# A two-layer float32 encoder trunk on one core: queueing edges in the second MLP product of layer 0 and in the attention output product, one weight cast moved ahead, and one activation table set for a norm's root and the softmax

## The chip, the core and the metric

The kernel runs on one core of one Trainium2 chip. The core has a matrix engine (TensorE; in the profile PE, its weight loads PEld), a vector engine (VectorE, DVE), an engine for activation functions and copies (ScalarE, ACT), a general engine (GpSimd, POOL) and an engine that only issues transfers (SyncE, SP). Each engine works through its own list of instructions in order; an instruction that depends on another engine waits on a semaphore, and everything behind it on the same engine waits too. The metric is the device time of one execution in microseconds (us).

## The reference

Two sequences of 512 tokens with 1024 features, `x_prompt` and `x_sample`, go through the same trunk. All is float32. Layer 0 mixes tokens with a 2-D Fourier transform and a product with `w_out`; layer 1 is attention with 8 query heads that share 2 key/value heads of 128 features. Each mixer is followed by an MLP with a squared ReLU.

```python
for i in range(2):
    if i == 0:
        x = x + fourier_mix(rms_norm(x, fourier_norm), fourier_w_out)
    else:
        x = x + gqa_attention(rms_norm(x, attn_norm), w_qkv, q_norm, k_norm, w_o)
    x = x + sq_relu_mlp(rms_norm(x, mlp_norm[i]), mlp_w_up[i], mlp_w_down[i])   # 1024 -> 4096 -> 1024
y = rms_norm(x, final_norm)

def rms_norm(x, g):
    return x * rsqrt(mean(x * x, axis=-1) + 1e-6) * g

def gqa_attention(h, w_qkv, q_gain, k_gain, w_o):     # per head
    q, k = axial_rope(rms_norm(q, q_gain)) * 128 ** -0.5, axial_rope(rms_norm(k, k_gain))
    return concat(softmax(q @ k.T) @ v) @ w_o
```

## The kernel before

**Products.** Each float32 operand is split into two reduced-precision halves: the high half is a cast on ACT (`split`, line 86; the page writes CAST L86), the low half is the difference to the source, a subtraction on DVE (line 87). A product is three matmuls: high by high, high by low, low by high (`mm3`, lines 81 to 83, in attention; `product`, line 907, elsewhere). Where float32 weights arrive by DMA, the tile is `raw`, its halves `w`; for activations both are `u`. PSUM banks are `ps`, eight of them. `halves` splits a whole weight tile of 128x1024 and returns two operands of 512 columns.

**Blocks.** Activations are kept transposed: features on partitions, tokens along the free axis. The MLP products and the product with W_o use Strassen's scheme over a 2x2 division (the two sequences are one of the divided sides): seven products of sums of blocks instead of eight. The class `Blocks` prepares the operands for the next layer's products: `gain` (line 206, ACT, multiplies by the norm's weight), `root` and `spread` (sums of squares, their root, and the root spread over partitions), `norm` (line 219, DVE, multiplies by the root), `first` (line 230, ACT, the high half) and `first_lo` (line 235, DVE, the low half), and `plain_sums` for the sums of blocks. `square` (lines 160 and 164) squares a feature block on ACT and adds it on POOL to a running sum.

**The order of a run.** The Fourier layer comes first; at its end (loop around line 870) every step adds one product to the residual, squares and scales it, and in some steps the MLP's first weight tiles are split. Then comes layer 0's first MLP product (`first_product`, results to DRAM), then its second (`second_product`), attention, W_o, layer 1's MLP and the final norm. Residuals that are not in use wait in DRAM (`park`; `put_away` writes, SP issues it).

**The second MLP product** works through items (a feature block m of four, a group of hidden rows g). In an item, PE runs the products of `Row` and `Sums`; meanwhile the weights of the next item are summed and split: after the product t3 the rows' casts, after t2 `sum_23` and `split_12`, after b22 `sum_4` and `split_4`, after t4 `split_3`, which makes the last pair of halves that the next item needs. When a block m has had its last item, `finish` adds the shared sum `e` to the residual (lines 1253 and 1254) and calls `ready(m)`. In layer 0, `ready` makes the attention layer's input (`make_h`: ACT line 90, DVE line 91), squares it, and puts the residual away.

**Attention.** `qkv` makes projections, `norm_rope` normalises each head of q and k by its root mean square and rotates it. The root comes from `rsqrt_steps`: Sqrt on ACT (line 136), a reciprocal and one Newton step on DVE. For the very last q tile, `norm_rope` is called with POOL as one of its engines; its steps are spread over the first heads. A loop over 16 heads then takes, for head n, four score tiles (`scores`: three matmuls, maximum on DVE, Exp on ACT line 1474, reciprocal on DVE, scaling on POOL), alternating with the transposition of the head before (`transpose_p`: four transposes on PE line 1482, a split on ACT and DVE), then transposes the next q (`transpose_q`, line 1461), then multiplies by the values (`values`; line 1499 copies the result). From the seventh head on, `load_kept` also loads and splits the first four W_o tiles, one half per step (line 1568): 8 halves. ACT needs a table for each function: a page's ACT_TABLE_LOAD is the load of one. After the loop, line 1682 issues a Sqrt whose only use is that its table is there for layer 1.

**The product with W_o** has a first, a middle and a last part; the last one takes the operands t1 and b22, adds each product to the residual (`add`, line 1688), squares and scales it, and between these begins the MLP's preparation for sequence 0: `root(0)`, `spread(0)`, `first(0)` to `first(3)`, `first_lo(0)` and `first_lo(1)`.

**What sets the order.** Inside `tc.manual_schedule(engines=...)` the named engines run in the order of the program text. Everywhere else a scheduler takes instructions by the order of the program and the modelled availability of their inputs, so the order on an engine can differ from that of the text. The Fourier loop above is ordered so, and so are ACT, DVE and POOL in the second MLP product and in the heads (there PE too); in the last part of W_o only PE follows the text. A dependency between two instructions can be added by hand; it then constrains this scheduler.

Of the kernel before, what the change touches and what calls it, by code (L numbers as in the profile page):

```python
# [19 lines left out]
P = 128  # L20
# [24 lines left out]
def trunk_kernel(ctx, tc, x_in, xt_in, y_out, tables, rope, gfour, gcol, grow, gfin,  # L45
# [39 lines left out]
    def split(dst_hi, dst_lo, src, eng=nc.vector):  # L85
        nc.scalar.copy(dst_hi, src)  # L86
        eng.tensor_sub(dst_lo, src, f32(dst_hi))  # L87
# [18 lines left out]
    def halves(raw, n=512, home=own):  # L106
        hi, lo = home()
        split(hi[:, : 2 * n], lo[:, : 2 * n], raw)
        return [(hi[:, i * n : (i + 1) * n], lo[:, i * n : (i + 1) * n]) for i in range(2)]
# [34 lines left out]

    xs, acc, apart = {}, {}, {}
# [9 lines left out]
    def square(q, fo, n=512, alone=False, first=0):  # L155

        if fo == first:
            acc[q] = tm()
        s = acc[q] if fo == first else tm()
        nc.scalar.activation(s[:, :n], xt(q, fo)[:, :n], AF.Square)  # L160
        if alone:
            apart[q] = s
        elif fo != first:
            nc.gpsimd.tensor_add(acc[q][:, :n], acc[q][:, :n], s[:, :n])  # L164

# [29 lines left out]
    class Blocks:  # L195
# [37 lines left out]
        def first_lo(self, i):  # L233
            h = self.b["b11" if i < 2 else "b21"][i % 2]
            nc.vector.tensor_sub(h[1], self.f[0, i], f32(h[0]))  # L235
# [466 lines left out]
    with tc.manual_schedule(engines={ET.PE, ET.Activation, ET.DVE, ET.Pool, ET.SP}):  # L702
# [163 lines left out]
        for fo in range(KC):  # L866
            odd_add(1, fo, odd_outs(1, [fo])[0])
            if fo == 7:
                rows.append(halves(raws[3]))
            if fo:  # L870
# [7 lines left out]
            if fo == 5:  # L878
                rows.append(halves(raws[2]))
# [214 lines left out]
    def second_product(l, blocks, rows, late=lambda: None, ready=lambda m: None):  # L1094
        e, new = [], [True] * 4
        there = set()
# [72 lines left out]
        class Sums:  # L1169
# [27 lines left out]
            def split_3(self):  # L1197
                self.s3, self.a22 = halves(self.y, self.n * P, (own, narrow)[self.n == 2])
# [51 lines left out]
        def finish(m):  # L1250
            left[m] -= 1
            if left[m] == 0:
                nc.vector.tensor_add(xs[0, m][:, 1], xs[0, m][:, 1], e[m])
                nc.vector.tensor_add(xs[1, m], xs[1, m], e[m].unsqueeze(1).broadcast_to([P, 2, 512]))
                ready(m)
# [107 lines left out]
    def ready(m):  # L1363
        for q in range(NSEQ):
            for fo in range(2 * m, 2 * m + 2):
                hT[q].append(make_h(q, fo, KC))
                square(q, fo)
            put_away(q, m)

# [32 lines left out]
    def norm_rope(raw, nh, table, ts, outs, ss=None, step=None, eng=nc.vector, scale=None):  # L1402
# [9 lines left out]
        steps = rsqrt_steps(r[:, :n], ss[:, :n], n, 1.0 / HD)  # L1412
# [32 lines left out]
    heads_out, ahead = Blocks(None), []  # L1445
# [33 lines left out]
    def transpose_p(probs, sc):  # L1479
# [4 lines left out]
        split(k[:, 0], k[:, 1], pt)  # L1484
        return k
# [65 lines left out]
    def load_kept():  # L1551
# [14 lines left out]
        for j in range(2 if i < 4 else 0):  # L1566
            yield
            split(*ahead[i][j], raw[:, j * 512 : j * 512 + 512])
# [79 lines left out]
    with tc.manual_schedule(engines={ET.Activation}):  # L1648
        o = qkv(1, 1, 2, ws[1])
        probs = [scores(*heads[0], first, t) for t in range(NT)]  # L1650
# [11 lines left out]
    for n in range(1, len(heads) + 1):  # L1662
        pts, nxt = [], []
        for t in range(NT):
            if n < len(heads):
                nxt.append(scores(*heads[n], qT, t))
            pts.append(transpose_p(probs, t))
# [19 lines left out]
    def add(x, o):  # L1687
        nc.vector.tensor_add(x, o, x)
# [9 lines left out]
    with tc.manual_schedule(engines={ET.PE}):  # L1698
# [38 lines left out]
        o = {}  # L1737
        for j, (m, i) in enumerate(turn()):
# [4 lines left out]
            add(xt(1, fo), o[m])  # L1743
# [10 lines left out]
            if 2 < j < 5:  # L1754
                blocks.first_lo(j - 3)
# [293 lines left out]
```

## Time and profile before

| | |
|---|---|
| three plain runs | 1680.02, 1680.24, 1682.67 us (median 1680.24) |
| profiled execution | 1682.5 us; its span 1680.5 us |
| instructions | 22279 |
| PE busy | 1666.0 us, 99% (7845 matmuls) |
| DVE busy | 1258.9 us, 75% |
| ACT busy | 873.4 us, 52% |
| POOL busy | 394.5 us, 23% |
| HBM | 218.11 MB read, 82.38 MB written, 179 GB/s over the span |

The span is the time from the first to the last instruction of the profiled execution; the execution's own time is 2.0 us longer. The table gives shares over the whole run, and says nothing of a single stage. A timeline row begins with the time at which a group of like instructions begins (us from the span's start), then their busy time, the engine, the line of the kernel, the operation, output and input tiles with their shapes, and the count; a bracket at the end gives idle time just before and what ended it. "u<-ps" is a tile u written from a PSUM bank.

Some places of this execution: the third Fourier weight tile (edit 1 below) is cast at 96.55 us, the last residual add of block 2 in layer 0 (edit 2) begins at 694.04, the activation table loads in the heads (edit 3) begin at 865.25 and 869.27, and the last part of W_o (edit 6) stands near 1046.

### The profile page before, as it was taken

To read this page: it belongs to the slowest core of one execution; us is meant where nothing else is said; L and a number is where in the kernel's file an instruction comes from. 1 tells how busy PE (TensorE), PEld (TensorE's weight loads), DVE (VectorE), ACT (ScalarE), POOL (GpSimd) and SP (SyncE) were. 2 spreads that over 40 slices of the span, in tenths; PEclk is the share of its full clock that TensorE was granted. 3 is DMA by queue.
4 is the path that set the end of the run, shared out by engine and by line. 5 is a ranking of instruction groups with operands and counts; after the bars stand their busy time and mean duration, and the time that the engine had idled before them with its cause. 6 is when DMAs were issued, how large, how long until landed. Compare 5 with 4: busy or idle time off the path is not lost.

```text
span 1680.5 us, 22279 instructions
## 1 busy us (share of the span) xinstructions
PE 1666.0 (99%) x7845; PEld 1387.7 (83%) x7845; DVE 1258.9 (75%) x1848; ACT 873.4 (52%) x1537; POOL 394.5 (23%) x364
## 2 busy tenths in 40 slices
PE   9999999999999999999999999999999999999998
PEld 8988888888888888788878888888888888888887
DVE  8879776557786779869888877777855487878865
ACT  6766444456343425447698854554544553433334
POOL 3321443221000001325544303004422220000002
PEclk9999999999999999999999999999999999999999
DMA  9843655459775757425501146334544696757532
GB/s 310 262 151 111 209 194 182 145 176 371 242 231 170 254 171 225 168 65 196 168 1 39 63 164 224 124 114 160 209 156 155 226 367 203 232 158 237 176 102 100
DMA packets 122047, 302.99 MB, mean 180 GB/s; under 512 B 12200, under 2 KB 13352, under 8 KB 121936
## 3 DMA queue, kind: packets, MB, share of 16 engines
q1 hardware_dynamic: 98576, 254.05, 43.6%
q0 software_dynamic: 8960, 21.05, 5.9%
q10 hardware_dynamic: 14400, 26.48, 4.2%
q8 instruction: 61, 1.00, 0.2%
q14 instruction: 50, 0.41, 0.1%
HBM read 218.11 MB, written 82.38 MB: 179 GB/s over the span
## 4 chain that ended last, share of the span: by engine, by line
PE 87%; DVE 6%; ACT 3%; issue 2%; DMA 2%; POOL 0%; SPq 0%; DVEq 0%; ACTq 0%; POOLq 0%
PE ps L907 69%; PE ps L83 5%; PE ps L81 5%; PE ps L82 5%; PE ps L1482 1%; DVE w L87 1%; ACT t L1474 1%; ACT u L86 1%; DVE u L87 1%; DVE u L219 1%; DVE u L235 1%; DVE u L1113 0%; DMA u<-w_four 0%; DMA u<-x 0%; PE ps L172 0%
## 5 line engine op out<-in xcount | busy, mean ns | idle before, releaser
L907 PE MATMUL ps<-u,w 128*128 128x512 f32 x4944 | 1133.3, 390 | 2.9 <-DVE w L87 2.1
L907 PEld LDWEIGHTS ps<-u,w 128*128 128x128 f32 x4944 | 927.5, 188 | 199.1 <-DVE w L87 3.2
L86 ACT CAST w<-raw 128x1024 fp32r<-128x1024 f32 (+1 forms) x216 | 214.0, 996 | 310.9 <-PE ps L907 229.0
L87 DVE TENSOR_TENSOR w<-raw,w 128x1024 fp32r<-128x1024 f32 (+1 forms) x216 | 252.3, 1172 | 77.6 <-ACT w L86 77.3
L86 ACT CAST u<-u 128x1024 fp32r<-128x1024 f32 x144 | 145.2, 1049 | 83.8 <-PE ps L907 36.5
L87 DVE TENSOR_TENSOR u<-u,u 128x1024 fp32r<-128x1024 f32 x144 | 173.3, 1230 | 19.0 <-ACT u L86 17.9
L907 PE MATMUL ps<-u,u 128*128 128x512 f32 x600 | 143.1, 389 | 0.1
L1142 POOL DMA_DIRECT2D raw<-w_sum x32 | 27.7, 866 | 469.3 <-DMA raw<-w_sum 197.9
L1113 DVE TENSOR_TENSOR u<-ps,u 128x512 f32<-128x512 f32 x160 | 109.6, 686 | 37.2 <-PE ps L907 34.4
L1023 POOL TENSOR_TENSOR u<-u 128x512 f32<-128x512 f32 x28 | 37.7, 1345 | 424.7 <-ACT u L920 424.7
L907 PEld LDWEIGHTS ps<-u,u 128*128 128x128 f32 x600 | 112.5, 188 | 23.8 <-ACT u L938 0.5
L81 PE MATMUL ps<-u,u 128*128 128x512 f32 (+2 forms) x340 | 128.8, 381 | 0.4 <-ACT t L1474 0.3
L82 PE MATMUL ps<-u,u 128*128 128x512 f32 (+2 forms) x340 | 124.2, 366 | 0.4 <-DVE u L87 0.3
L83 PE MATMUL ps<-u,u 128*128 128x512 f32 (+2 forms) x340 | 124.4, 366 | 0.1
L164 POOL TENSOR_TENSOR t<-t,t 128x512 f32<-128x512 f32 (+1 forms) x54 | 77.8, 1446 | 190.6 <-ACT t L160 189.9
L919 ACT ACTIVATE t<-t 128x512 f32<-128x512 f32 x64 | 40.5, 632 | 109.8 <-DVE t L992 99.8
L87 DVE TENSOR_TENSOR u<-ps,u 128x512 fp32r<-128x512 f32 (+3 forms) x112 | 68.5, 635 | 7.9 <-ACT u L86 7.3
L83 PEld LDWEIGHTS ps<-u,u 128*128 128x128 f32 x340 | 64.2, 189 | 10.5 <-DVE u L448 0.5
L81 PEld LDWEIGHTS ps<-u,u 128*128 128x128 f32 x340 | 64.3, 189 | 10.1 <-ACT u L86 1.5
L82 PEld LDWEIGHTS ps<-u,u 128*128 128x128 f32 x340 | 64.4, 189 | 9.2 <-DVE u L87 1.4
L979 DVE TENSOR_TENSOR t<-ps,u 128x512 f32<-128x512 f32 x32 | 22.0, 688 | 60.5 <-PE ps L907 52.7
L1476 POOL TENSOR_SCALAR t<-t,s 128x512 f32<-128x512 f32 x64 | 47.3, 740 | 74.0 <-DVE s L1475 60.1
(260 smaller groups left out, 2029.7 us busy)
## 6 DMA issues: line engine op xcount, KB each, us to landing
raw<-w_up SPq DMA_DIRECT2D x80, 512.0 KB, 4.6
u<-spill_t SPq DMA_DIRECT2D x60, 512.0 KB, 6.8
raw<-w_sum SPq DMA_DIRECT2D x56, 512.0 KB, 5.7
u<-spill_b SPq DMA_DIRECT2D x45, 512.0 KB, 6.2
spill_t<-u SPq DMA_DIRECT2D x84, 256.0 KB, 2.0
spill_b<-t ACTq DMA_DIRECT2D x60, 256.0 KB, 4.3
raw<-w_row SPq DMA_DIRECT2D x28, 512.0 KB, 5.2
park<-u SPq DMA_DIRECT2D x24, 512.0 KB, 4.5
```

Source lines behind the costliest of these rows:

```text
L81: nc.tensor.matmul(out, lh, rh, start=first, stop=False)
L82: nc.tensor.matmul(out, lh, rl, start=False, stop=False)
L83: nc.tensor.matmul(out, ll, rh, start=False, stop=last)
L86: nc.scalar.copy(dst_hi, src)
L87: eng.tensor_sub(dst_lo, src, f32(dst_hi))
L164: nc.gpsimd.tensor_add(acc[q][:, :n], acc[q][:, :n], s[:, :n])
L907: nc.tensor.matmul(o, w[x][:, sl], h[k][y], start=first and k + i == 0, stop=k == n - 1 and i == 2, skip_group_check=not first)
L919: nc.scalar.activation(t, src, AF.Relu)
L1023: eng.tensor_sub(t[:, 0], b12, b11)
L1113: nc.vector.tensor_add(x, o, x)
L1142: nc.gpsimd.dma_start(s[:, 1], w[:, 3], accum_op=ALU.add)
L1476: nc.gpsimd.tensor_scalar(p, p, sm_[:, :1], 1.0, ALU.mult, ALU.mult)
```

## The change

It has six edits.

1. At the end of the Fourier layer the split of the third weight tile, `halves(raws[2])` at step 5, stands ahead of that step's square and gain instead of behind them.
2. `behind(x, y)` is a new helper: instruction x may only come after y, as an order (no semaphore) or, with `sync=True`, as a wait. In `second_product` of layer 0, when block m = 2 is finished, the last residual add (line 1254) is placed behind the low half that the next item's `split_3` makes last, and six squares (the last two of block 1, and block 2's four) are placed behind the same low half with a wait.
3. A new `log_steps` computes the root by Ln and Exp(-0.5 x) instead of Sqrt and a reciprocal, with the same Newton step; `norm_rope` uses it in the one call that names POOL.
4. Before the first softmax the table set that holds both Ln and Exp is loaded.
5. The splits of W_o's first four tiles in the heads are remembered in `fresh`; one is taken at the fourth `transpose_p` of a head and placed behind that transposition's own split, cast behind cast and subtraction behind subtraction.
6. In the last part of W_o the low halves of `first_lo(0)` and `first_lo(1)` are placed behind the residual adds of steps 4 and 5.

To allow this, `split`, `square`, `first_lo`, `ready` and `add` return the instructions that they issue, and `halves` takes a function to be called with its low half.

```diff
@@ -83,8 +83,14 @@
         nc.tensor.matmul(out, ll, rh, start=False, stop=last)
 
     def split(dst_hi, dst_lo, src, eng=nc.vector):
-        nc.scalar.copy(dst_hi, src)
-        eng.tensor_sub(dst_lo, src, f32(dst_hi))
+        hi = nc.scalar.copy(dst_hi, src)
+        return hi, eng.tensor_sub(dst_lo, src, f32(dst_hi))
+
+    def behind(x, y, sync=False):
+
+        kind = mybir.DependencyClass.Sync if sync else mybir.DependencyClass.NoSync
+        tc.add_manual_dep(x.ins, y.ins.name, mybir.DependencyInfo(kind, mybir.DependencyReason.SCHED_ONLY),
+                          reason="order")
 
     def split_scaled(dst_hi, dst_lo, src, scale):
         nc.scalar.activation(dst_hi, src, AF.Copy, scale=scale)
@@ -103,9 +109,9 @@
         w = slot([P, 2, 512], F32R)
         return w[:, 0], w[:, 1]
 
-    def halves(raw, n=512, home=own):
+    def halves(raw, n=512, home=own, done=lambda x: None):
         hi, lo = home()
-        split(hi[:, : 2 * n], lo[:, : 2 * n], raw)
+        done(split(hi[:, : 2 * n], lo[:, : 2 * n], raw)[1])
         return [(hi[:, i * n : (i + 1) * n], lo[:, i * n : (i + 1) * n]) for i in range(2)]
 
     def lent():
@@ -142,6 +148,18 @@
 
 
 
+    def log_steps(out, ss, n, inv):
+
+        v, s, r, t = [small(n)[:, :n] for _ in range(4)]
+        return [
+            lambda: nc.vector.tensor_scalar(v, ss, inv, EPS, ALU.mult, ALU.add),
+            lambda: nc.scalar.activation(s, ss, AF.Ln, scale=inv, bias=eps[:, :1]),
+            lambda: nc.scalar.activation(r, s, AF.Exp, scale=-0.5),
+            lambda: nc.vector.tensor_mul(t, r, r),
+            lambda: nc.vector.scalar_tensor_tensor(t, t, -0.5, v, ALU.mult, ALU.mult),
+            lambda: nc.vector.scalar_tensor_tensor(out, t, 1.5, r, ALU.add, ALU.mult),
+        ]
+
     xs, acc, apart = {}, {}, {}
 
     def load_xs(q, src):
@@ -157,11 +175,12 @@
         if fo == first:
             acc[q] = tm()
         s = acc[q] if fo == first else tm()
-        nc.scalar.activation(s[:, :n], xt(q, fo)[:, :n], AF.Square)
+        made = nc.scalar.activation(s[:, :n], xt(q, fo)[:, :n], AF.Square)
         if alone:
             apart[q] = s
         elif fo != first:
             nc.gpsimd.tensor_add(acc[q][:, :n], acc[q][:, :n], s[:, :n])
+        return made
 
     def sums(q, n=NT):
 
@@ -232,7 +251,7 @@
 
         def first_lo(self, i):
             h = self.b["b11" if i < 2 else "b21"][i % 2]
-            nc.vector.tensor_sub(h[1], self.f[0, i], f32(h[0]))
+            return nc.vector.tensor_sub(h[1], self.f[0, i], f32(h[0]))
 
         def plain_sums(self):
 
@@ -867,6 +886,8 @@
             odd_add(1, fo, odd_outs(1, [fo])[0])
             if fo == 7:
                 rows.append(halves(raws[3]))
+            if fo == 5:
+                rows.append(halves(raws[2]))
             if fo:
                 square(1, fo - 1)
             if fo > 1:
@@ -875,8 +896,6 @@
                 rows.append(halves(raws[fo]))
             if 1 < fo < 4:
                 blocks.first_lo(fo)
-            if fo == 5:
-                rows.append(halves(raws[2]))
         square(1, KC - 1)
         for fo in range(KC - 2, KC):
             gain1(fo)
@@ -1093,7 +1112,7 @@
 
     def second_product(l, blocks, rows, late=lambda: None, ready=lambda m: None):
         e, new = [], [True] * 4
-        there = set()
+        there, owed = set(), []
 
         def fetch(op, g, n):
 
@@ -1195,7 +1214,8 @@
                 split(*self.s4, self.x[:, 0])
 
             def split_3(self):
-                self.s3, self.a22 = halves(self.y, self.n * P, (own, narrow)[self.n == 2])
+                self.s3, self.a22 = halves(self.y, self.n * P, (own, narrow)[self.n == 2],
+                                           lambda x: setattr(self, "low", x))
 
             def go(self, i):
                 m, x0, x1 = self.m, xs[0, self.m], xs[1, self.m]
@@ -1251,8 +1271,14 @@
             left[m] -= 1
             if left[m] == 0:
                 nc.vector.tensor_add(xs[0, m][:, 1], xs[0, m][:, 1], e[m])
-                nc.vector.tensor_add(xs[1, m], xs[1, m], e[m].unsqueeze(1).broadcast_to([P, 2, 512]))
-                ready(m)
+                x = nc.vector.tensor_add(xs[1, m], xs[1, m], e[m].unsqueeze(1).broadcast_to([P, 2, 512]))
+                made = ready(m)
+                if m == 1 and made:
+                    owed.extend(made[2:])
+                if m == 2 and made:
+                    behind(x, items[-1][1].low)
+                    for y in owed + made:
+                        behind(y, items[-1][1].low, True)
 
         first_product(l, blocks, rows, ahead)
         e += [tm() for _ in range(4)]
@@ -1361,11 +1387,13 @@
         split(*wkv[-1], raw)
 
     def ready(m):
+        made = []
         for q in range(NSEQ):
             for fo in range(2 * m, 2 * m + 2):
                 hT[q].append(make_h(q, fo, KC))
-                square(q, fo)
+                made.append(square(q, fo))
             put_away(q, m)
+        return made
 
     second_product(0, blocks, rows, late, ready)
 
@@ -1409,7 +1437,7 @@
             head_squares(raw, 0, n, ss, 1.0 if scale is None else scale)
             yield
         r = small(n)
-        steps = rsqrt_steps(r[:, :n], ss[:, :n], n, 1.0 / HD)
+        steps = (log_steps if eng is nc.gpsimd else rsqrt_steps)(r[:, :n], ss[:, :n], n, 1.0 / HD)
         steps[0]()
         yield
         steps[1]()
@@ -1442,7 +1470,7 @@
             yield
 
     vt, kr, kT, qr = {}, {}, {}, {}
-    heads_out, ahead = Blocks(None), []
+    heads_out, ahead, fresh = Blocks(None), [], []
 
     def transpose_k(q):
         for h in range(NKV):
@@ -1481,8 +1509,7 @@
         for t in range(NT):
             nc.tensor.transpose(pt[:, t * P : (t + 1) * P], probs[t][:, sc * P : (sc + 1) * P], ident)
         k = slot([P, 2, 512], F32R)
-        split(k[:, 0], k[:, 1], pt)
-        return k
+        return k, split(k[:, 0], k[:, 1], pt)
 
     def values(q, h, pts):
         o = ps()
@@ -1565,7 +1592,7 @@
         ahead.append([(w[0][:, c : c + 512], w[1][:, c : c + 512]) for c in (0, 512)])
         for j in range(2 if i < 4 else 0):
             yield
-            split(*ahead[i][j], raw[:, j * 512 : j * 512 + 512])
+            fresh.append(split(*ahead[i][j], raw[:, j * 512 : j * 512 + 512]))
 
 
     transposes = {(0, 0, 0): 0, (0, 1, 0): 1}
@@ -1647,6 +1674,7 @@
     raw, ss = slot([P, 1024], F32), small(8)
     with tc.manual_schedule(engines={ET.Activation}):
         o = qkv(1, 1, 2, ws[1])
+        tc.keep_in_program_order(nc.scalar.preload_act_table_set("natural_log_exp_and_others"))
         probs = [scores(*heads[0], first, t) for t in range(NT)]
         nc.scalar.activation(raw[:, :512], o, AF.Copy, scale=rs[1][:, 2:3])
         qT = transpose_q(*heads[1])
@@ -1664,7 +1692,12 @@
         for t in range(NT):
             if n < len(heads):
                 nxt.append(scores(*heads[n], qT, t))
-            pts.append(transpose_p(probs, t))
+            k, both = transpose_p(probs, t)
+            pts.append(k)
+            if t == NT - 1:
+                for x in (fresh.pop() if fresh else ()), :
+                    for a, b in zip(x, both):
+                        behind(a, b)
             if n > 2 and t == 0:
                 for _ in range(3 if n == 3 else 1):
                     next(todo, None)
@@ -1685,7 +1718,7 @@
     load_xs(0, park[0])
 
     def add(x, o):
-        nc.vector.tensor_add(x, o, x)
+        return nc.vector.tensor_add(x, o, x)
 
     def turn(*steps):
 
@@ -1734,13 +1767,15 @@
                 next(todo, None)
                 if k == 2 and m < 2:
                     rows.append(halves(load_raw(w_up[1, 2 * m]), home=lent))
-        o = {}
+        o, lows = {}, []
         for j, (m, i) in enumerate(turn()):
             if i == 0:
                 o[m] = ps()
             product(o[m], ahead[10 + m][i], heads_out.operand(("t1", "b22")[i]), i == 0)
             fo = 2 * m + 1 - i
-            add(xt(1, fo), o[m])
+            added = add(xt(1, fo), o[m])
+            if 3 < j < 6:
+                behind(lows[j - 4], added)
             square(1, fo, first=1)
             blocks.gain(1, fo)
             if i:
@@ -1752,7 +1787,7 @@
             if 1 < j < 6:
                 blocks.first(j - 2)
             if 2 < j < 5:
-                blocks.first_lo(j - 3)
+                lows.append(blocks.first_lo(j - 3))
         for i in range(2, 4):
             blocks.first_lo(i)
     second_product(1, blocks, rows)
```

## The prediction

> **What bounds the kernel now.** I read the page first, then PE's busy time, matmuls and clock in chosen stretches, then the timeline of each engine where PE falls behind.
>
> ```profile
> span 1680.5 us, 22279 instructions
> PE 1666.0 (99%) x7845; PEld 1387.7 (83%) x7845; DVE 1258.9 (75%) x1848; ACT 873.4 (52%) x1537; POOL 394.5 (23%) x364
> ```
>
> PE bounds the kernel: it is busy for 1666.0 of 1680.5 us. No part of the change takes a matmul away, so only PE's waits can be gained, and 14.5 us of idle time, with what hides in overlapping records, is all there is. Matmul records overlap, so the counts show what busy time hides.
>
> ```profile
> 120.00:160.00 40.00, 40.00 (x176) 1.00 0.22 79
> 697.70:701.10 3.40, 3.40 (x9) 0.50 0.90 241
> 851.06:866.51 15.45, 15.45 (x90) 1.00 0.01 2
> 866.51:884.00 17.49, 16.72 (x91) 1.00 0.00 1
> 907.38:954.93 47.55, 47.30 (x266) 1.00 0.17 56
> 1340.00:1360.00 20.00, 20.00 (x90) 1.00 1.04 400
> ```
>
> Columns: stretch and length, PE's busy time and matmuls, granted clock, DMA share, GB/s. Undisturbed, a 128x512 product starts every 40.00/176 = 0.227 us. The attention windows are cut where a head begins (the transposes of line 1461): two undisturbed heads take 15.45 us (7.73 each), the next two 17.49 (2.0 lost), six later ones 47.55 against 46.35 (1.2 lost).
>
> The profiled execution took 1682.5 us (2.0 around its span). The three plain runs have a median of 1680.24 and reach from 1680.02 to 1682.67, so the profile stands 2.3 above the median, inside the spread. The sum is made against 1682.5 and then carried to the median.
>
> **1. The cast sooner (line 878, end of the Fourier layer).** The cast of the third row weight moves in ACT's order ahead of one square and one gain.
>
> ```profile
> 93.71 0.71 ACT L206 ACTIVATE u<-u,gc 128x512 f32<-128x512 f32 x1
> 96.55 1.04 ACT L86 CAST w<-raw 128x1024 fp32r<-128x1024 f32 x1
> 95.57 0.40 DVE L683 TENSOR_TENSOR u<-u,ps 128x255 f32<-128x255 f32 x1
> 97.63 1.23 DVE L87 TENSOR_TENSOR w<-raw,w 128x1024 fp32r<-128x1024 f32 x1 [1.65 <-ACT w L86]
> 92.64 6.08 PE L907 MATMUL ps<-u,w 128*128 128x512 f32 x26
> 98.91 3.47 PE L907 MATMUL ps<-u,w 128*128 128x512 f32 x14 [0.19 <-DVE w L87]
> ```
>
> PE's 26 starts end at 92.64 + 25 x 0.227 = 98.3; the next belongs at 98.55 and comes at 98.91, and the 14 after it take 0.13 more than their pace: 0.5 lost. The cast can begin at 94.42, when the gain ends; DVE's low half then runs at 96.0 (after line 683) and ends at 97.2. The square and the gain run after it; the 1.65 us that DVE waited shows the room, and PE waits for neither. The whole 0.5 goes (bounds 0, were the next operand late instead, and 0.8). Two matmuls of the fourth pair change places; that costs nothing.
>
> **2. Edges in layer 0's second product.** `behind` puts the last low half of weights (line 87) before the m = 2 residual sum (line 1254), and six squares behind that low half: three were ahead of the weights' casts.
>
> ```profile
> 684.33 2.18 ACT L160 ACTIVATE t<-u 128x512 f32<-128x512 f32 x4
> 688.79 1.56 ACT L86 CAST w<-raw 128x512 fp32r<-128x512 f32 x2
> 685.09 7.77 POOL L164 TENSOR_TENSOR t<-t,t 128x512 f32<-128x512 f32 x4 [14.58 <-ACT t L160]
> 687.69 2.31 DVE L87 TENSOR_TENSOR w<-raw,w 128x1024 fp32r<-128x1024 f32 x1
> 689.93 1.78 DVE L91 SCALAR_TENSOR_TENSOR u<-u,gc,u 128x512 fp32r<-128x512 f32 x1
> 694.04 1.22 DVE L1254 TENSOR_TENSOR u<-u,t 128x1024 f32<-128x1024 f32 x1
> 695.19 1.22 DVE L87 TENSOR_TENSOR w<-raw,w 128x1024 fp32r<-128x1024 f32 x1
> 687.82 6.74 PE L907 MATMUL ps<-u,w 128*128 128x512 f32 x29
> 696.46 7.81 PE L907 MATMUL ps<-u,w 128*128 128x512 f32 x26 [1.91 <-DVE w L87]
> ```
>
> PE's 29th start is at 687.82 + 28 x 0.227 = 694.2; the 30th belongs at 694.4 and comes at 696.46: 2.05 lost. The 26 after it should take 25 x 0.227 + 0.39 = 6.07 and take 7.81: 1.7 more, because the clock is 0.50 for 3.4 us after that wait (window above). Together 3.8 us.
>
> Moving the low half before line 1254 ends it 1.22 earlier, at 695.2. The rest comes from the squares: with three of four gone, POOL stops near 687 instead of 692.9, and DVE's operations beside it shrink: line 87 takes 2.31 there and 1.22 at 695.19, with POOL idle. By the same ratio line 91's 1.78 becomes 0.94. That gives back 1.1 and 0.8; the casts, done by 688.79 + 1.56 = 690.35, do not hold it. The low half then ends at 693.3, 1.1 ahead of PE, and I take 3.8. The lower bound is 1.2: only the one move counts and the half clock stays.
>
> Queued behind the new wait on ACT are the three squares, then gains; POOL's sums of squares follow them, six of 1.9 (7.77 over four) at most, and PE reads them only after the products still to come. What is late next is the residual add that must read the first bank before PE reuses it, 24 products after 694.2, at 699.6: it is the fifth DVE operation behind the low half, the first of them 1.22 long, so it ends near 697.5, or near 700 if POOL stretches them as it does now. SP issues one w_qkv load ahead of a residual put-away; the load only starts earlier, the put-away has no reader near.
>
> **3. One table set (`log_steps`, line 1410).** Ln and Exp take the place of Sqrt and a reciprocal; the table load before the first softmax only changes its set, the two inside attention go.
>
> ```profile
> 865.25 1.28 ACT L136 ACT_TABLE_LOAD   x1
> 866.54 0.30 ACT L136 ACTIVATE s<-s,eps 128x8 f32<-128x8 f32 x1
> 866.75 1.54 ACT L86 CAST u<-ps 128x512 fp32r<-128x512 f32 x3
> 869.27 1.28 ACT L1474 ACT_TABLE_LOAD   x1
> ```
>
> ACT loses two loads, 2.57 us, and gains one activation of 0.30: 2.3 less in a stretch where it has no slack, while PE loses 2.0 there. The eight scalings of line 1427 remain and crowd one head, so I take 1.6 (bounds 0 and 2.0). The Trainium skill ("ScalarE: Activation LUTs", "What ACT_TABLE_LOAD costs") gives 1283 ns for the load plus about 1380 ns of drain per switch, an estimate of 5.3 us of ACT for two. The trace agrees on the load; no drain stands in it (ACTIVATE starts 0.01 us after), and PE's loss caps this term anyway.
>
> **4. W_o's splits later.** Each of eight half splits now stands behind the last cast of the next head's probabilities.
>
> ```profile
> 909.28 0.65 ACT L86 CAST w<-u 128x512 fp32r<-128x512 f32 x1
> 910.46 0.65 ACT L86 CAST w<-u 128x512 fp32r<-128x512 f32 x1
> 911.51 0.47 PE L81 MATMUL ps<-u,u 128*128 128x512 f32 x1
> 912.09 0.33 PE L1482 MATMUL ps<-ident,t 128*128 128x128 f32 x1
> ```
>
> Two casts in one head hold up exponentials, and PE waits 0.3 at 912.09: the 1.2 of the six heads. One per head still holds up the last two exponentials and the next q's cast by 0.65, while PE's new order defers the last block's transpose by two products (0.45). About 0.1 per head remains: 0.5 gained, between 1.2 gained and 0.4 lost.
>
> **5. A side effect at the end of attention.** In the changed kernel's order the Sqrt that preloads for layer 1 (line 1682) and its load move ahead of the four last casts.
>
> ```profile
> 965.93 0.59 ACT L1499 COPY u<-ps 128x512 f32<-128x512 f32 x1 [0.72 <-PE ps L83]
> 966.69 2.05 ACT L86 CAST u<-ps 128x512 fp32r<-128x512 f32 x4 [0.17 <-PE ps L1482]
> 968.76 1.28 ACT L1682 ACT_TABLE_LOAD   x1
> 967.72 0.47 PE L81 MATMUL ps<-u,u 128*128 128x512 f32 x1
> ```
>
> Now the load hides behind PE's values. Afterwards it runs from 966.5 to 967.8, the Sqrt to 968.0, and the first cast ends at 968.6 instead of 967.3; PE, ready at 967.7, waits 0.9. Three W_o matmuls, put forward, fill 0.2 of later waits: 0.7 lost (0 to 1.3).
>
> **6. Edges in the W_o product.** The low halves of the first two operands (line 235) go behind two adds.
>
> ```profile
> 1042.62 2.31 DVE L235 TENSOR_TENSOR u<-u,u 128x1024 fp32r<-128x1024 f32 x1
> 1044.85 0.68 DVE L1688 TENSOR_TENSOR u<-ps,u 128x512 f32<-128x512 f32 x1
> 1045.45 1.21 DVE L235 TENSOR_TENSOR u<-u,u 128x1024 fp32r<-128x1024 f32 x1
> 1047.19 1.69 DVE L219 TENSOR_TENSOR u<-u,t 128x1024 f32<-128x1024 f32 x1
> 1047.32 3.02 PE L907 MATMUL ps<-u,w 128*128 128x512 f32 x12 [0.73 <-DVE u L1688]
> ```
>
> DVE has no idle time here. Before the add that PE waits for, one 1.21 row leaves and the norm of line 219 (1.69) is drawn forward, so that add hardly moves; only overlaps with POOL shift, and a later wait may go. I take 0.4 gained, between 1.3 (both waits) and 0.3 lost.
>
> **Sum.** -0.5 - 3.8 - 1.6 - 0.5 + 0.7 - 0.4 = -6.1 us against 1682.5: 1676.4. Carried to the median it is 1674.1 if the plain runs hold the same waits. If the runs near 1680.2 owe their lead to a start of PE without the half clock (1.7 of the 2.3), the gain there is 4.4: 1675.8. I forecast 1675.0.
>
> **The rivals.** *A. The half clock is chance* (1675.8, chance 0.14). For it: plain runs lie 2.4 apart, near the 1.7. Against: the profile has it right after the wait. The Trainium skill ("TensorE: Matmul & The Clock Gate", "What's actually happening") has the clock halved after an idle window of 3.4 us that runs freely. By that rule a wait of 2.3 need not halve it; the trace shows that it did here.
>
> *B. A new wait in step 2.* The half clock stays and the bank's add lands at 700.6 beside POOL: step 2 gives 1.2 - 1.0 = 0.2, the sum is -2.5 and the time 1677.7. For it: POOL's four sums lie where they now stretch DVE. Against: the margin of 2 us if they don't. Chance 0.14.
>
> *C. The gain is given back.* Near 1340 the DMA share is 1.04; if those transfers start no earlier, PE arrives early and waits: near 1680.2. Against: PE is undisturbed there (90 matmuls in 20 us). Chance 0.10.
>
> *D. Slower.* If a W_o split's cast (0.65) and its low half (0.68 by the add row) both stand in line in each of eight heads, step 4 costs 10.6 instead of gaining 0.5: 1682.5 - 5.6 + 10.6 = 1687.5, or 1685.2 at the median. It decides from 0.7 per head on. Against: the two-cast head lost only 0.3. Chance 0.05.
>
> The forecast itself has 0.57. Faster takes the forecast and A; B and C are within 0.2% (3.4 us, about what a measurement can tell from no change), D is slower. The terms' bounds add up to -9.1 at best (1671.1) and +0.8 at worst (1681.0); 1671.5 to 1680.0, just inside them, leaves out D, the end of C and the far tails, some 2 in 10.
>
> **What would show it.** PE's row near 694 runs on without a wait and without the 0.50 window; the two heads from 866.5 take under 16 us with one activation load, none on line 136; the heads of 907 to 955 take 46.5 to 47; PE waits 0.7 to 0.9 before the last head's values; the add that ends PE's 0.73 wait near 1047 still does. Wrong would be: a wait of over 1 us at the bank's add, heads over 8 us, or a clock that halves in the tail of attention.

## The result and the profile after

The changed kernel takes 1678.38 us (median of 22 runs, 1676.65 to 1680.46); the kernel before takes 1680.77 us (22 runs, 1679.15 to 1685.5). The ratio is 0.9986, with a 95% interval from 0.9981 to 0.9992: 2.4 us faster, between 1.3 and 3.2, and so faster, but by less than the 0.2% that the prediction set as its bound. The forecast was 1675.0 us in a range of 1671.5 to 1680.0. The profiled execution took 1678.77 us, 3.7 less than that of before.

The page of the changed kernel, and its busy time in chosen stretches (columns as in the prediction: stretch and length, PE's busy time and matmuls, granted clock, DMA share, GB/s):

```profile
span 1677.0 us, 22277 instructions
PE 1664.0 (99%) x7845; PEld 1387.3 (83%) x7845; DVE 1261.1 (75%) x1847; ACT 870.0 (52%) x1536; POOL 395.0 (24%) x364
```

```profile
690.00:697.00 7.00, 7.00 (x33) 1.00 0.86 261
697.70:701.10 3.40, 3.40 (x17) 1.00 0.55 224
846.60:862.10 15.50, 15.50 (x91) 1.00 0.01 2
862.10:878.13 16.03, 15.86 (x90) 1.00 0.01 1
901.80:948.96 47.16, 47.15 (x266) 1.00 0.14 46
```

PE no longer stops near 694, and the clock stays at 1.00 behind it, where before had 9 matmuls in 3.4 us there are 17. The two heads with the last norm take 16.03 us instead of 17.49, the six later ones 47.16 instead of 47.55.

To see where the rest went, I numbered PE's 7845 matmuls in order of their starts, in every profile, and took the time from one number to another. A stretch that PE runs at full pace has the same length in every profile; a longer one holds a wait. These are the stretches that the edits touch, and one more that differs; `again`, `third` and `fourth` are further profiles of the same kernel. The first 640 matmuls, which wait for the first loads, are left out (89.67 to 90.61 us in the four profiles of before, 89.51 and 90.08 in the two after):

```
matmuls     near us  before  again   third   fourth | after   again
 640- 720     91     17.06   17.05   17.07   17.07  | 16.56   16.56   edit 1, the cast
3280-3360    688     21.95   19.61   20.39   19.28  | 18.13   18.13   edit 2, layer 0's edges
4060-4250    859     36.07   36.02   36.03   36.04  | 34.89   34.92   edits 3, 4, the table set
4250-4300    895      8.81    8.82    8.83    8.82  |  8.92    8.91
4300-4640    904     61.49   61.47   61.40   61.49  | 60.80   60.79   edits 3, 4 and 5
4640-4700    966     12.31   12.32   12.32   12.30  | 13.05   13.09   the end of attention
4980-5030   1039     12.37   12.37   12.36   12.37  | 12.88   12.89   edit 6, W_o's last part
5030-5100   1052     16.29   16.29   16.31   16.27  | 16.03   16.03
7100-7300   1521     45.42   46.64   48.32   45.33  | 47.06   45.47   no edit
```

Between the two profiles that were compared first, the stretches give -0.50, -3.82, -1.18, +0.11, -0.69, +0.74, +0.51, -0.26 and +1.64: -3.45 us, which is the 3.5 by which the span is shorter. Between profiles of one kernel these stretches differ by at most 0.1 us, except two: the one near 688 in the kernel before, and the one near 1521 in both kernels. Outside the table the two profiles that were compared first agree within 0.05 us a stretch, but for the first 640 matmuls; the third profile of before has 0.5 us more between matmuls 720 and 3280.

### The profile page after: what moved, and what is told of

Same layout as the page of the kernel before. It is cut to its first block, busy times and chain, and to the rows that moved or that the text cites. A ratio compares the mean times of both kernels' runs of the same rounds, so it can differ in the third digit from the quotient of the medians.

```text
span 1677.0 us, 22277 instructions
## 1 busy us (share of the span) xinstructions
PE 1664.0 (99%) x7845; PEld 1387.3 (83%) x7845; DVE 1261.1 (75%) x1847; ACT 870.0 (52%) x1536; POOL 395.0 (24%) x364
## 4 chain that ended last, share of the span: by engine, by line
PE 94%; DVE 2%; DMA 2%; ACT 1%; issue 1%; SPq 0%; POOL 0%; DVEq 0%; ACTq 0%; POOLq 0%
PE ps L926 71%; PE ps L83 6%; PE ps L81 6%; PE ps L82 6%; PE ps L1510 2%; DMA raw<-w_sum 1%; DVE u L87 0%; DMA u<-x 0%; DMA u<-w_four 0%; PE ps L1489 0%; PE ps L191 0%; DVE u L238 0%; PE ps L495 0%; DMA u<-spill_t 0%; PE ps L492 0%
## 5 line engine op out<-in xcount | busy, mean ns | idle before, releaser
L1468 POOL TENSOR_TENSOR u<-t,t 128x256 f32<-128x256 f32 x40 | 49.0, 1237 | 62.9 <-DVE t L1466 43.4
```

The costliest lines, as they stand in the source:

```text
L1468: nc.gpsimd.tensor_add(outs[(h0 + i) // 2].rearrange("p (h d) -> p h d", h=2), t1[:, i : i + 2], t2[:, i : i + 2])
```

## The experiments

### Is the half clock, and with it 1.7 of step 2, always there?

The kernel before was profiled three more times, and once with the wait made longer: the last low half of weights (line 87) also behind line 1253.

> The kernel before, unchanged, profiled a second time. If the half clock after line 87's wait in layer 0 belongs to the wait, PE again waits about 2 us near 694 and then runs 3.4 us at 0.50 (1.7 us more). If it is chance, the wait is there and the clock stays at 1.00, and the execution comes out about 1.7 us shorter, near 1680.8. Near 1520 to 1555 the first profile lost nothing to transfers; if the 1.65 us that the changed kernel lost there is chance, this run may lose some too.

> The kernel before, profiled a third time. So far PE's step over the wait near 694 was 2.30 us with the half clock after it (21.95 us for matmuls 3280 to 3360) and 1.55 without it (19.61). If the wait alone decides, a step of 1.5 goes without and one of 2.3 with the half clock; if it is chance, no such order. The same pair of values tells what edit 2 can gain in the typical run: 1.5 or 3.8.

> As the third profile. Four profiles then say how often the kernel before pays the half clock: the plain runs, whose median lies 1.7 below the first profile, speak for seldom.

```diff
-                nc.vector.tensor_add(xs[0, m][:, 1], xs[0, m][:, 1], e[m])
+                x0 = nc.vector.tensor_add(xs[0, m][:, 1], xs[0, m][:, 1], e[m])
...
+                if m == 2 and made:
+                    behind(items[-1][1].low, x0)
```

> Before, with line 87's last low half put behind one more add and line 1253: PE's wait near 694 grows by 1.3 to about 3.0 to 3.4 us. If a longer wait brings the half clock, the clock is 0.50 for 3.4 us after it and matmuls 3280 to 3360 take about 23.3; if it is chance, 21.6 without it is as likely.

PE's timeline at the wait, in the second profile of before, the third, and with the longer wait, in this order:

```profile
696.38 5.98 PE L907 MATMUL ps<-u,w 128*128 128x512 f32 x25 [1.16 <-DVE w L87]
```

```profile
697.88 4.42 PE L907 MATMUL ps<-u,w 128*128 128x512 f32 x18 [1.92 <-DVE w L87]
```

```profile
697.47 6.70 PE L926 MATMUL ps<-u,w 128*128 128x512 f32 x22 [2.50 <-DVE w L87]
```

And the stretch behind the wait in the same three, with the granted clock third from the end:

```profile
697.70:701.10 3.40, 3.40 (x17) 1.00 0.93 270
```

```profile
698.00:701.40 3.40, 3.40 (x15) 1.00 0.87 298
```

```profile
697.50:700.80 3.30, 3.30 (x8) 0.54 0.97 335
```

The steps over the wait, from one matmul's start to the next, are 2.30 us in the first profile of before, then 1.55, 2.31 and 1.24, and 2.89 with the longer wait. Only the first of these and the last have the half clock behind them. The longer wait grew by 0.6 us, not by the 1.3 that was expected. The third profile waits as long as the first (1.92 against 1.91 us idle) and keeps the full clock, so the wait's length alone does not decide: the half clock came in one of four profiles of before, and the sum was made on that one. The time of an execution does not tell which kind it was: the three without the half clock took 1681.98, 1685.00 and 1680.66 us, the one with it 1682.5, because they also differ by up to 3 us near 1521.

The traces show what decides together with the length. From its first full value, 4.2 to 6.7 us after the span's start, the granted clock changes only at whole multiples of 3.413 us (203 of them before the half clock in the first profile, one for the half clock, 286 after it), so each execution has its own grid of such windows. In the first profile the 1.91 us of idle time all fall into one window (694.26 to 697.68), and with the longer wait 2.13 of the 2.50 (693.68 to 697.10); the half clock begins where that window ends. In the third profile a boundary at 697.18 cuts the wait into 1.22 and 0.70. In the second and the fourth, one window holds 1.16 and 0.85. In all thirteen profiles no other window up to the last matmul has more than 1.51 us without a matmul, and no other is followed by the half clock. So what counts here is the idle time within one window, with a bound between 1.51 and 1.91 us, and where the wait falls on the grid differs between executions.

The Trainium skill ("TensorE: Matmul & The Clock Gate", "What's actually happening") has a window of 3413 ns that runs freely, not started by the kernel. The trace agrees with that part: equal waits with and without the half clock, and a half clock of about 3.4 us when it comes. It names an idle window of about 3.4 us as the condition; here 1.91 us of idle time within one window were followed by it, and the measurement decides.

### Which part of edit 2 does it?

> Before, with the edges of layer 0's second product alone (edit 2). My step 2: PE runs past 694 without a wait and without half clock, 3.8 us earlier from 701 on in the profile; in time 3.8 less if the kernel before always pays the half clock, 2.1 if it is chance in the plain runs, and less by up to 1.6 if the end of layer 1's second product (1520 to 1555) gives back what comes early. Rival (the gain is not this edit's): under 1 us at 701.

The kernel before with edit 2 alone took 1679.81 us beside 1680.78 for before (11 and 15 runs), a ratio of 0.9995 with an interval from 0.9986 to 1.0005. Its stretch near 688 is 18.13 us, as in the changed kernel. In the profile that is the 3.8 of my step; in time it is between 2.4 gained and 0.8 lost, which excludes 3.8 and agrees with the 1.2 to 2.3 that the three profiles of before without the half clock lose at this wait.

Then each kind of edge by itself, of these lines:

```diff
+                    behind(x, items[-1][1].low)
+                    for y in owed + made:
+                        behind(y, items[-1][1].low, True)
```

The first line alone, the residual add:

> Before, with only the edge that puts the m = 2 residual add behind the last low half; the squares stay ahead of the casts. My step: the low half loses the 1.22 us of the add and no more, ends near 695.2, and PE still waits about 0.8 to 1.1 with the subtractions beside POOL at 2.3 us. Rival (the order of the add is everything): PE does not wait at 694.

The other two alone, the squares:

> Before, with only the edge that puts six squares behind the last low half; the residual add stays ahead of it. My step: line 87's 2.31 us near 688 becomes 1.2 and line 91's 1.78 becomes 0.75 to 0.94, so the low half ends 1.9 to 2.1 us earlier, near 694.4, and PE waits under 0.4 us. Rival (POOL's sums do not stretch DVE, the add is everything): PE still waits 2 us.

DVE and PE with the add's edge alone, and then with the squares' edges alone:

```profile
687.04 2.31 DVE L87 TENSOR_TENSOR w<-raw,w 128x1024 fp32r<-128x1024 f32 x1
693.26 1.21 DVE L87 TENSOR_TENSOR w<-raw,w 128x1024 fp32r<-128x1024 f32 x1
675.75 26.54 PE L926 MATMUL ps<-u,w 128*128 128x512 f32 x116
```

```profile
688.50 1.21 DVE L87 TENSOR_TENSOR w<-raw,w 128x1024 fp32r<-128x1024 f32 x1
693.35 1.22 DVE L87 TENSOR_TENSOR w<-raw,w 128x1024 fp32r<-128x1024 f32 x1
681.46 20.72 PE L926 MATMUL ps<-u,w 128*128 128x512 f32 x90 [0.33 <-DVE w L87]
```

In the first, POOL's four sums still stretch the subtraction to 2.31; in the second it takes 1.21, as the step had it. But the last low half ends at 694.47 and at 694.57, and PE runs on past it in both (18.22 and 18.13 us for the stretch). My step gave the add alone an end near 695.2 and a wait of 0.8 to 1.1: that did not come. In that run all of DVE's work there stands 0.65 earlier than in the first profile of before (line 87's 2.31 begins at 687.04 instead of 687.69); in the other, PE comes 0.8 later. Each kind of edge was enough in its one run: with the add's alone the low half ends 0.1 us before PE's next start (694.56), with the squares' alone 0.6 before it (695.21). That does not show that the add's edge is always enough. In the first and third profiles of before the low half ends 2.24 and 2.26 us after the last start ahead of PE's wait, in the others 1.49 and 1.19; the add's edge brought it forward by 1.28, so by these numbers a wait of about 0.75 would have been left in two of the four (an estimate). Together they leave room, as the changed kernel's DVE shows, with POOL's row behind it:

```profile
690.48 1.22 DVE L87 TENSOR_TENSOR w<-raw,w 128x1024 fp32r<-128x1024 f32 x1
691.61 1.22 DVE L1274 TENSOR_TENSOR u<-u,t 128x1024 f32<-128x1024 f32 x1
694.46 1.79 DVE L97 SCALAR_TENSOR_TENSOR u<-u,gc,u 128x512 fp32r<-128x512 f32 x1
696.17 1.47 DVE L1132 TENSOR_TENSOR u<-ps,u 128x512 f32<-128x512 f32 x2
```

```profile
692.50 11.13 POOL L182 TENSOR_TENSOR t<-t,t 128x512 f32<-128x512 f32 x7 [6.47 <-ACT t L178]
```

The low half ends at 691.7, two microseconds before PE wants it. The seven sums that POOL now makes from 692.5 on stretch line 97 to 1.79, and the bank's add still ends by 697.64, and PE does not wait.

### Which edit costs the end of attention, and which the last part of W_o?

Edit 5 was taken back, and in another run edit 6 alone:

```diff
-                for x in (fresh.pop() if fresh else ()), :
-                    for a, b in zip(x, both):
-                        behind(a, b)
```

> After without edit 5: W_o's splits go back to where the scheduler puts them. My steps 4 and 5: the heads between matmuls 4300 and 4640 take 61.1 to 61.5 instead of 60.80 (0.35 to 0.7 lost), the tail 12.3 instead of 13.05 (0.7 gained), since by the order the table load moves only with this edit; the time within 0.5 us of after. Rival (the tail load moves with the table set): the tail stays at 13.05.

```diff
-            if 3 < j < 6:
-                behind(lows[j - 4], added)
```

> After without edit 6. If the edges themselves cost the 0.51 us between matmuls 4980 and 5030 (12.88 against 12.37), it is 12.37 again; if the order that edit 5 leaves costs it, it stays near 12.88. The 0.26 gained between 5030 and 5100 (16.03 against 16.29) goes with the edges, in my step 6.

A second run of the changed kernel stood beside them:

> The changed kernel unchanged, a second profile and times beside the three below. In its first profile PE loses 1.73 us between its 7100th and 7300th matmul (45.33 us at full pace), where DVE waits for weight sums from DRAM. If that is given back because PE comes 5.3 us early, it is there again, 1.5 to 1.9; if it is chance in the transfers, anything from 0 to 1.7, as the five profiles so far have it (0.09, 1.31, 0.00, 0.82, 0.80).

```
matmuls     before  after   again   without 5   without 6
4300-4640   61.49   60.80   60.79   61.21       60.79
4640-4700   12.31   13.05   13.09   12.29       13.03
4980-5030   12.37   12.88   12.89   12.89       12.37
5030-5100   16.29   16.03   16.03   16.03       16.27
7100-7300   45.42   47.06   45.47   47.11       45.38
```

Edit 5 gains 0.42 in the heads and loses 0.75 at the end of attention: the table load moves with it, and not with the table set. Of the 0.69 gained in the heads, 0.27 is left for edits 3 and 4. The second run of the changed kernel took 1678.40, the one without edit 5 1678.94, both at 0.9988 of before (0.9979 to 0.9997). By the stretches the one without edit 5 should be 0.33 faster; a difference of that size cannot be told in time. Edit 6 loses 0.51 and gains 0.25; without it both stretches are those of before. The stretch near 1521 was 45.47 this time: what the first profile of the changed kernel lost there is not a fixed price of coming early.

ACT and PE of the changed kernel at the end of attention:

```profile
959.74 0.58 ACT L1526 COPY u<-ps 128x512 f32<-128x512 f32 x1 [0.43 <-PE ps L83]
960.35 1.28 ACT L1715 ACT_TABLE_LOAD   x1
961.64 0.20 ACT L1715 ACTIVATE s<-t 128x1 f32<-128x1 f32 x1
961.75 2.03 ACT L86 CAST u<-ps 128x512 fp32r<-128x512 f32 x4
```

```profile
962.37 0.50 PE L81 MATMUL ps<-u,u 128*128 128x512 f32 x1 [0.43 <-ACT u L86]
962.71 0.86 PE L926 MATMUL ps<-u,w 128*128 128x512 f32 x3
```

The load stands right in front of the casts, as the prediction had it, and PE waits for the first cast; the three W_o matmuls were drawn in behind it. Ahead of it PE has a second new wait, inside the last head's 16 transposes, for the last scaling of probabilities on POOL:

```profile
960.63 1.31 PE L1510 MATMUL ps<-ident,t 128*128 128x128 f32 x10 [0.27 <-POOL t L1504]
```

In before and without edit 5 the 16 transposes run through without a wait; in before they stand here:

```profile
965.73 2.23 PE L1482 MATMUL ps<-ident,t 128*128 128x128 f32 x16
```

With edit 5 the last W_o split stands in front of the last exponential on ACT (a cast of 0.63) and of the last reciprocal on DVE (a low half of 0.89). DVE and PE of the changed kernel in the last part of W_o, and PE without edit 6:

```profile
1037.77 1.72 DVE L254 TENSOR_TENSOR u<-u,u 128x1024 fp32r<-128x1024 f32 x1
1039.41 2.32 DVE L238 TENSOR_TENSOR u<-u,t 128x1024 f32<-128x1024 f32 x1
1041.65 0.68 DVE L1721 TENSOR_TENSOR u<-ps,u 128x512 f32<-128x512 f32 x1
```

```profile
1042.38 3.02 PE L926 MATMUL ps<-u,w 128*128 128x512 f32 x12 [1.25 <-DVE u L1721]
```

```profile
1043.36 3.02 PE L926 MATMUL ps<-u,w 128*128 128x512 f32 x12 [0.73 <-DVE u L1721]
```

Ahead of the second add stand now a low half of 1.72 and the norm (line 238) of 2.32, where before had low halves of 2.31 and 1.21: half a microsecond more, and PE's wait grows from 0.73 to 1.25. The norm's row in before is 1.69; at its new place this sum on POOL runs beside it:

```profile
1039.17 1.48 POOL L182 TENSOR_TENSOR t<-t,t 128x512 f32<-128x512 f32 x1 [0.77 <-ACT t L178]
```

### Both orders put right

```diff
-    nc.scalar.activation(one[:, :1], last[:, :1], AF.Sqrt)
+    behind(nc.scalar.activation(one[:, :1], last[:, :1], AF.Sqrt), last_cast)
...
             if 1 < j < 6:
-                blocks.first(j - 2)
+                made = blocks.first(j - 2)
+                if j == 5:
+                    behind(made, added)
+                    hold.append(added)
...
-                self.row = halves(self.raw)
+                self.row = halves(self.raw, done=lambda x: behind(x, hold[0]) if hold and self.p == 3 else None)
```

`last_cast` is the cast of the last `transpose_p`; `first` returns its norm, and the low half of the fourth weight row goes behind the same add as the norm.

> After, with two orders put right: the Sqrt of line 1715 and its load behind the last cast of the last head, and in the last part of W_o the norm of the fourth block and the split of the fourth weight row behind the add that PE waits for. My step 5 (the load ahead of the casts is what PE waits for): the 13.05 us between matmuls 4640 and 4700 become 12.3, as in before. My reading of the W_o wait (the norm drawn forward, 2.32, holds the add): the 12.88 between 4980 and 5030 become 12.0 to 12.4. In all 1.2 to 1.6 us less than after. Rival (PE waits for something else there, next in line): the first or the second stays above 12.8, and the time does not move.

Its DVE, PE and ACT at the two places:

```profile
1037.46 1.72 DVE L255 TENSOR_TENSOR u<-u,u 128x1024 fp32r<-128x1024 f32 x1
1039.10 0.68 DVE L1725 TENSOR_TENSOR u<-ps,u 128x512 f32<-128x512 f32 x1
1041.34 2.32 DVE L238 TENSOR_TENSOR u<-u,t 128x1024 f32<-128x1024 f32 x1
```

```profile
1029.67 13.88 PE L927 MATMUL ps<-u,w 128*128 128x512 f32 x60
```

```profile
961.16 2.06 ACT L86 CAST u<-ps 128x512 fp32r<-128x512 f32 x4 [0.64 <-PE ps L1513]
963.74 1.28 ACT L1719 ACT_TABLE_LOAD   x1
```

The add now ends at 1039.8, and PE's 60 matmuls run through without a wait: the stretch takes 11.33 us, 50 steps at full pace, 1.0 less than in before, too. The stretch behind it takes 16.27, as in before, so 0.24 of that goes back. The two edges there were not run one by one; by the rows it is the norm's 2.32 that left the place in front of the add. The end of attention takes 12.55 instead of 13.05, not the 12.3 expected: the first cast now waits for PE's transposes, and these still wait 0.24 for POOL. In all the stretches gain 1.8 us on the changed kernel, where 1.2 to 1.6 was expected. The kernel took 1676.12 us (6 runs, 1675.59 to 1678.68), 0.9970 of before (0.9959 to 0.9982). Changed and unchanged kernel stood at 1678.40 and 1681.33 beside it: it beats both, by 2.3 and 5.2 us, and it is the version to keep.

## Why the prediction was right, and where it was not

The time lies inside the range, but 3.4 us above the forecast, between the times of rivals B (1677.7) and C (1680.2), whose mechanisms no run shows. That it is inside is owed to a range of 8.5 us as much as to the steps. Of the 3.4 us, 0.5 is the median of before, 1680.24 with three runs and 1680.77 with 22; the rest is gain, 5.2 forecast and 2.4 measured.

Of the signs that the prediction named, PE's row near 694 came. The first two heads took 16.03 us (under 16 was named), the later ones 47.16 (46.5 to 47), PE's wait for the last casts is 0.43 (0.7 to 0.9), and the add near 1047 ends a wait of 1.25 in place of 0.73. Of the signs of being wrong, one came in part: the head from 862.10 still takes 8.31 us (8.52 in before), where over 8 was named; the others did not. Edits 1, 3 and 4 were not run alone: the stretches at 91 and 859 us move in every run that has them and in no other.

*Step 1* (0.5): 0.50. The cast runs at 94.18, the low half at 95.75, and PE runs past it, as these rows of ACT, DVE and PE in the changed kernel show:

```profile
94.18 1.03 ACT L86 CAST w<-raw 128x1024 fp32r<-128x1024 f32 x1
```

```profile
95.75 1.21 DVE L87 TENSOR_TENSOR w<-raw,w 128x1024 fp32r<-128x1024 f32 x1
```

```profile
92.47 10.84 PE L926 MATMUL ps<-u,w 128*128 128x512 f32 x47
```

*Step 2* (3.8): 3.82 against the profile that the sum was made on, and that is the step that failed for the time. That the half clock stood "right after the wait" was taken as a cause that acts in every execution, and rival A (the half clock is chance, 1675.8, 0.14) as unlikely. The half clock stands in one of four profiles, where the wait falls into one window of 3.413 us; without it, the three others put the gain at 1.48, 2.26 and 1.15. The remark that plain runs lie 2.4 us apart was the better evidence. The mechanism was right in its parts (the add's move, POOL's stretch gone: 2.31 became 1.21), its bound for the add alone did not come: one run with it had no wait, though by the times of the first profile it would have had one.

*Step 3* (1.6): 1.07 in the first heads and 0.27 in the later ones, 1.3 to 1.4 in all. One load before the softmax, none on the root. Ln and Exp follow each other without a load, so a load brings a set of functions, and not one function's table:

```profile
831.45 1.28 ACT L1677 ACT_TABLE_LOAD   x1
860.60 0.38 ACT L156 ACTIVATE s<-s,eps 128x8 f32<-128x8 f32 x1
861.01 0.21 ACT L157 ACTIVATE s<-s 128x8 f32<-128x8 f32 x1
```

*Step 4* (0.5): 0.42 by taking edit 5 back. The size came out with some luck: the step's own 0.65 and 0.45 leave 0.2 per head and not 0.1, and six times 0.2 would have eaten the 1.2. Rival D (a split that costs over 0.7 per head) is out.

*Step 5* (-0.7): -0.75, at the place named, but only 0.50 comes back when the load goes behind the casts. The other 0.25 fits the wait for POOL's last scaling, which the step did not see, so the sum came out partly by luck.

*Step 6* (0.4 gained): 0.25 lost, inside the step's bounds. The step saw the norm drawn ahead and one low half leave, and called the add's place hardly moved. Its own prices, 1.69 in and 1.21 out, already put the add 0.48 later, and it came 0.52 later. The norm took 2.32 at its new place and not 1.69, but the low half that stayed took 1.72 and not 2.31, which cancels. The later wait that might go was worth 0.25.

*Rival B* (a new wait at the bank's add) is out: the add ends at 697.64. *Rival C* (given back to transfers) named the stretch near 1340, where nothing was lost, but there is such a place near 1521 to 1555. DVE waits there for weight sums from DRAM, and adds that free PE's banks stand behind that wait. In the changed kernel's first profile:

```profile
1518.46 0.43 DVE L1202 TENSOR_TENSOR raw<-raw,raw 128x256 f32<-128x256 f32 x1 [2.16 <-DMA raw<-w_sum]
1545.06 0.69 DVE L1202 TENSOR_TENSOR raw<-raw,raw 128x512 f32<-128x512 f32 x1 [1.94 <-DMA raw<-w_sum]
```

```profile
1548.27 3.03 PE L926 MATMUL ps<-u,w 128*128 128x512 f32 x12 [0.44 <-DVE t L1132]
```

and in the third profile of before, DVE and then PE:

```profile
1551.30 0.69 DVE L1183 TENSOR_TENSOR raw<-raw,raw 128x512 f32<-128x512 f32 x1 [3.59 <-DMA raw<-w_sum]
```

```profile
1554.51 3.04 PE L907 MATMUL ps<-u,w 128*128 128x512 f32 x12 [2.09 <-DVE t L1113]
```

Beyond the 45.33 us of full pace (200 steps of 0.2267), eight profiles (four of before, three with edit 2 or a part of it, and the longer wait) lost 0.96 on average there (0.00 to 2.99), the five of the changed kernel and its variants 0.75 (0.03 to 1.78). So no lead is seen to be given back, though with values that scatter so widely up to about 1 us could hide (an estimate from the scatter): the transfers arrive just in time, sometimes late, in either kernel.

The account for the profiles: the sum was -6.1, the span moved by -3.5. Of the 2.6 between, 1.64 is the transfers' lateness in that one profile, 0.65 step 6, 0.25 step 3, 0.1 steps 4 and 5. The account for the medians: with the mean of the three profiles of before without the half clock (19.76 us) step 2 is worth 1.6, and the sum is -0.5 - 1.6 - 1.35 - 0.42 + 0.75 + 0.25 = -2.9 us, inside the interval of -3.2 to -1.3. With the first profile's 3.8 it would be -5.1, outside; with all four profiles' mean, 2.2, it would be -3.5, just outside, and four profiles do not fix how often the half clock comes. The 0.5 that is left to the measured -2.4 isn't explained by any run.

## What to carry to other kernels

A profile is one execution: before a wait and what follows it go into a sum, profile the unchanged kernel again, because 1.7 of the 6.1 us forecast here, and 1.6 of what then seemed to be missing, were things that come and go between executions. For the clock, add up the idle time that can fall into one window of the clock's grid, and not the length of the wait alone. An edge that holds one instruction back lets the scheduler draw another forward: read the new order for each edge, add up every row that then stands in front of what the bottleneck waits for (half a microsecond was passed over here), and where something lands there that need not, place a second edge; three such edges took another 2.3 us off the 2.9 that the whole change gave beside them. Cost a stalled operand against the moment at which it is wanted in several profiles, since both moved by over half a microsecond.

## What was not expected of the hardware

Two waits of the same length (idle 1.91 and 1.92 us) were followed by the half clock in one execution and not in the other: the first lay in one window of 3.413 us, the other was cut by a boundary into 1.22 and 0.70. Less than two microseconds of idle time in a window were enough. The same transfers at the same place cost PE between 0.00 and 2.99 us in different executions of one kernel.
